# A hybrid diffusion-transformer layer: wide and narrow matmuls issued in two streams, and one PSUM pool of bank pairs for the whole program

## The chip, the cores and the metric

The kernel runs on 1 core of one Trainium2 chip, in one launch. Its time is device microseconds; the time before is the median of 3 runs, 1769.75 us (1761.52 to 1772.15). TensorE is PE in all rows (PEld is its weight load), VectorE is DVE, ScalarE is ACT, GpSimd is POOL, and SyncE, which only issues DMAs here, is SP.

## The reference, cut to what matters

One layer over 256 latent tokens of width 2048, with 256 context tokens as a prefix, all in float32:

```python
mod = silu(c) @ w_mod + b_mod                    # 6 vectors: shift, scale, gate, twice
h   = modulate(rms_norm(x), sh1, sc1)            # and hc for the context
q, zf, zb, v = split(h @ w_in[:, :4096], 4)      # HGRN2, both directions, 8 heads
o   = scan_f(q, zf, v) + scan_b(q, zb, v)        # chunkwise gated recurrence
g, sb, sc, sh, ga, gb = split(h @ w_in[:, 4096:])
y_a = rms(o) * a_norm_g * silu(g);  y_b = sb * short_conv(sc * sh)
x   = x + g1 * ((sigmoid(ga) * (y_a @ w_pa) + sigmoid(gb) * (y_b @ w_pb)) @ w_o)
a, b = split(modulate(rms_norm(x), sh2, sc2) @ w_up, 2)       # 5632 columns each
x   = x + g2 * ((silu(dwconv3x3(a) + db) * b) @ w_down)
return rms_norm(x) * final_g
```

## The kernel before

**Products in split form.** Each float32 weight block is loaded by SP into a tile `raw` (1 MB, 4 buffers, L66), and `wsplit` (L83) makes two tiles of 1024 columns of it twice: `w_hi` on ACT (L95), the weight rounded to the matmul's format, and `w_lo` on DVE (L96), what is left over. 5 buffers of each stand ahead of PE. The activations are kept split in the same way: `hx[:, k, 0]` is the high part of row tile k of h, `hx[:, k, 1]` the low part, 256 tokens each, next to each other. A product is w_hi times high, w_hi times low, and w_lo times high.

**The projections** (`proj`, L364; `proj_q`, L381, the same for q): the weights are the stationary operand, 128 x 128, and tokens move. For a row tile k and a half n of 256 columns, `mm2` (L123) issues a wide matmul, `w_hi` over high and low together (512 columns, one PSUM bank), and right behind it a narrow one, `w_lo` over the high part (256 columns), which adds to the second half of that bank. The order is thus wide, narrow, wide, narrow, in 64 matmuls for 16 row tiles and two halves. `joined` (L129) then adds the two halves of a bank: an ACT copy and a DVE addition. There are 4 projections for q, 16 for the rest of the token mixer, 16 for the gates and 44 in the FFN, and 16 of half the length on `w_pa` and `w_pb`.

**Other products.** `proj_xc` (L395) makes forget gates from narrow matmuls alone, `values` (L442) and `token_product` (L755) have the activations stationary and the weights moving. `token_product` gives the two products at the end, w_o and w_down, in 4 column quarters `cq` of 512; t is one of two tiles of 128 tokens. In the last quarter t = 0 is finished first, then the two 256-column pieces of t = 1, and `residual` (L797) adds each to x (L804, L805), squares it (L807) and takes the root for the norm (L811, L812). After w_o the norm's factor goes through a matmul into `rb` and multiplies the transposed rows (L838 to L865), after w_down it scales the output (L943 to L947), which leaves in 8 DMAs (L948).

**PSUM.** 8 banks: `psH` has 2 for small things; the other 6 change hands between pools, 6 single banks (`psA` to L629, `psB` L739 to L875, `psD` from L918) or 3 pairs (`psW` L630 to L738, `psF` L876 to L917). A pool's tile waits until what stood in its banks in the pool before has been read.

**The order of the work.** A scheduler of the framework lays out each engine's queue from the order of the code and its own timing model; each engine then runs its queue in order and waits at semaphores. SP's queue of loads is fixed by it too. The stages, by the trace: norm, modulation and first gates to about 155 us, HGRN2 with its projections to about 432 (its last group's vector work runs on beyond), the mixer's and the gates' projections to about 940, w_o to 1010, the FFN's two projections to 1517, w_down to the end. `mod_steps` (L646) runs the remaining modulation on DVE beside the mixer and the FFN, with 16 one-column products (twice, L115 `pc`).

Of the kernel before, what the change touches and what calls it, by code (L numbers as in the profile page):

```python
# [36 lines left out]
def hybrid_layer_kernel(ctx: ExitStack, tc: tile.TileContext, I, out, dbg=None):  # L37
# [17 lines left out]
    def banks(name, n):  # L55
        cm = tc.tile_pool(name=name, bufs=n, space=PSUM, reuse_waits="tile")
        return cm, cm.__enter__()

    psA_cm, psA = banks("psA", 6)

# [56 lines left out]
    def mm3(o, wl, wh, sl, sh, start, stop):  # L117
# [3 lines left out]
        mm(o, wh, sl, False, stop)  # L121

    def mm2(o, wl, wh, s, start, stop):  # L123


        mm(o, wh, s, start, False)
        mm(o[:, T:2 * T], wl, s[:, 0, :], False, stop)

# [97 lines left out]
    for i in range(2):  # L226
        for t in range(2):
            for j, part in enumerate(xts[2 * i + t]):
                nc.scalar.activation(junk, part, AF.Square, accum_out=ssq[:, j, 2 * i + t:2 * i + t + 1])
        r = rstd[:, 2 * i:2 * i + 2]  # L230
        nc.vector.tensor_tensor(out=r, in0=ssq[:, 0, 2 * i:2 * i + 2], in1=ssq[:, 1, 2 * i:2 * i + 2], op=ALU.add)
        nc.scalar.activation(r, r, AF.Sqrt, scale=1.0 / D, bias=eps_t[:])
        nc.vector.reciprocal(r, r)
        for t in range(2):
            for part in xts[2 * i + t]:
                nc.vector.tensor_scalar(out=part, in0=part, scalar1=rstd[:, 2 * i + t:2 * i + t + 1], scalar2=None, op0=ALU.mult)
            for k4 in range(4):
                pt = psA.tile([P, 4, P], F32, name="pt4", tag="acc")
                for k in range(4):
                    kk = 4 * (k4 % 2) + k  # L240
                    nc.tensor.transpose(pt[:, k, :], xts[2 * i + t][k4 // 2][:, kk * P:kk * P + P], ident[:])  # L241
                if k4 % 2:
                    nc.scalar.copy(xsT[:, 4 * k4:4 * k4 + 4, 2 * i + t, :], pt[:])
                else:
                    nc.vector.tensor_copy(xsT[:, 4 * k4:4 * k4 + 4, 2 * i + t, :], pt[:])

# [6 lines left out]
    zacc = {}  # L253
    for d, n in [(0, n) for n in range(4)] + [(1, n) for n in range(3)]:
        pool, tag = (psH, "psh") if (d, n) == (0, 0) else (psA, "acc")
        zt = pool.tile([P, 2, T], F32, name=f"zacc{d}{n}", tag=tag)
        zacc[d, n] = zt

# [105 lines left out]
    def proj(w, cols, src, kt):  # L364

        accs = []
        for i in range(len(cols)):
            acc = psW.tile([P, 2, 2, T], F32, name="acc", tag="acw")
            accs.append(acc)
# [9 lines left out]
        return accs  # L379

    def proj_q(c0):  # L381

        accs = []
        for n in range(2):
            acc = psA.tile([P, 2, T], F32, name="acc", tag="acc")
            accs.append(acc)
        for c in range(2):
            for k, hv, lv in wviews([wblock(w_in, c * 1024, 8, c0, 256)], 8):
                kk = 8 * c + k
                for n in range(2):  # L390
                    mm2(accs[n][:].rearrange("p a b -> p (a b)"), lv[:, n * P:n * P + P], hv[:, n * P:n * P + P],
                        hx[:, kk], kk == 0, kk == KD - 1)
        return accs

    def proj_xc(w, cols):  # L395

        accs = []
        for n in range(2):
            a = psA.tile([P, 2, T], F32, name=f"acx{n}", tag="acc")
            accs.append(a)  # L400
        for c in range(2):
# [8 lines left out]
    def proj_xc1(w, c0):  # L410

        acc = psA.tile([P, 2, T], F32, name="acx", tag="acc")
        for k, hv, lv in wviews([wblock(w, 0, KD, c0, P)], KD):
# [14 lines left out]
    def gate_evac(acc, dst):  # L428

        nc.scalar.activation(dst, acc[:], AF.Sigmoid)  # L430

    def q_evac(accs):
        q = gp.tile([P, 2, T], F32, name="q", tag="q", bufs=2)
        for n, acc in enumerate(accs):
            nc.scalar.copy(q[:, n, :], acc[:, 1, :])
            nc.vector.tensor_tensor(out=q[:, n, :], in0=acc[:, 0, :], in1=q[:, n, :], op=ALU.add)  # L436
        sg = g2.tile([P, 2, T], F32, name="sq", tag="qq")
# [4 lines left out]
    def values(cb):  # L442
        accs = []
        for t in range(4):
            a = psA.tile([P, 512], F32, name=f"vacc{t}", tag="acc")
            accs.append(a)
        for c4 in range(4):
            for k, hv, lv in wviews([wblock(w_in, c4 * 512, 4, 3 * AW + cb * 512, 512)], 4):
                kk = 4 * c4 + k
                for t in range(4):  # L450
                    h = hx if t < 2 else hc
                    ts = slice((t % 2) * P, (t % 2) * P + P)
                    mm(accs[t][:], h[:, kk, 0, ts], hv, kk == 0, False)
                    mm(accs[t][:], h[:, kk, 0, ts], lv, False, False)
                    mm(accs[t][:], h[:, kk, 1, ts], hv, False, kk == KD - 1)
        for t in range(4):
            nc.scalar.copy(v[:, t, cb * 512:cb * 512 + 512], accs[t][:])

# [142 lines left out]
    for g in range(4):  # L601
# [135 lines left out]
    tp_cm.__exit__(None, None, None)  # L737
    psW_cm.__exit__(None, None, None)  # L738
    psA_cm, psA = banks("psB", 6)  # L739


# [89 lines left out]
    for cq in range(4):  # L831
        accs = token_product(w_o, KD, cq, mg_part)
        norm2 = residual(accs, cq, bcast[2], tw)
        if cq == 3:
            rb = psA.tile([P, T], F32, name="rb", tag="acc")
            for t in range(2):
# [15 lines left out]
    dump("x1", x1[:])  # L852
    rbv = strided(rb[:], 0, [[0, 2], [1, T]])
    h2_hi = {}
# [19 lines left out]

    psA_cm.__exit__(None, None, None)  # L875
    psW_cm, psW = banks("psF", 3)  # L876
    yfp = ctx.enter_context(tc.tile_pool(name="yfp", bufs=1, reuse_waits="tile"))
# [38 lines left out]
    pump(1)  # L916
    psW_cm.__exit__(None, None, None)  # L917
    psA_cm, psA = banks("psD", 6)  # L918

# [18 lines left out]
    for t in range(2):  # L938
        for cq in (0, 1, 3, 2):
# [8 lines left out]
            nc.sync.dma_start(out[0, t * P:t * P + P, cs], v1)  # L948
    psA_cm.__exit__(None, None, None)

# [35 lines left out]
```

## Time and profile before

| what | us |
|---|---|
| median of 3 runs | 1769.75 |
| the profiled execution, its own time | 1774.06 |
| span of its instructions | 1772.3 |
| PE busy in it | 1731.1 |
| DVE busy | 1317.2 |
| ACT busy | 895.5 |

The profiled execution is 4.3 us above the median; its time is 1.8 us more than its span. A matmul's duration in a row is its whole way through the array, and matmuls overlap; what one costs in a stream is the distance from its start to the start of the next.

### The profile page before, as it was taken

Reading aid. Unit: us, or ns where it says so; the run is one execution under the profiler, and the core shown is the slowest. Engines: PE = TensorE matmul, PEld = TensorE weight load, DVE = VectorE, ACT = ScalarE, POOL = GpSimd, SP = SyncE. Lnnn points to the kernel's source line nnn. Section 1 sums busy time; section 2 is a strip of 40 time slices with the busy share of each in tenths; the row PEclk is TensorE's granted clock in tenths of the full one; section 3 lists DMA queues with packets and bytes.
Section 4 is the critical chain, followed back from the end, with each engine's and each line's share of the span. In section 5 each row is a group of like instructions: output and inputs, shape, how many; then the busy total and the mean of one; then the engine's idle time right before and its main releaser. Section 6 shows DMA issues by size and latency. Waiting matters only on the chain.

```text
span 1772.3 us, 25752 instructions
## 1 busy us (share of the span) xinstructions
PE 1731.1 (98%) x10391; PEld 1493.0 (84%) x10391; DVE 1317.2 (74%) x1693; ACT 895.5 (51%) x1142; POOL 21.4 (1%) x26
## 2 busy tenths in 40 slices
PE   5999999998999999999999999999999999999998
PEld 3778888997888888888888888888888888788887
DVE  4337377687988778878875588888888887877774
ACT  4227356466555444444455454444444454665653
POOL 0000000000000000000000000000000000000000
PEclk9999999999999999999999999999999999999999
DMA  9996224223677879979886367777777755566662
GB/s 334 352 329 208 95 72 119 72 96 120 223 252 253 275 245 312 323 258 327 295 292 223 119 214 238 237 231 228 233 235 237 237 193 188 166 191 192 197 191 85
DMA packets 288989, 384.96 MB, mean 217 GB/s; under 512 B 7812, under 2 KB 241581, under 8 KB 280038
## 3 DMA queue, kind: packets, MB, share of 16 engines
q1 hardware_dynamic: 287872, 379.82, 65.1%
q10 hardware_dynamic: 694, 3.24, 0.5%
q8 instruction: 81, 1.33, 0.3%
q0 software_dynamic: 304, 0.26, 0.1%
q14 instruction: 38, 0.31, 0.0%
HBM read 381.20 MB, written 2.10 MB: 216 GB/s over the span
## 4 chain that ended last, share of the span: by engine, by line
PE 97%; DVE 1%; ACT 0%; DMA 0%; issue 0%; SPq 0%; ACTq 0%
PE acc L115 56%; PE to L115 19%; PE acx L115 6%; PE vacc L115 5%; PE zacc L115 5%; PE pm L115 2%; PE ps L115 2%; PE po L115 1%; PE pt L241 1%; DMA xt<-in_x_dram 0%; DVE w_lo L96 0%; PE pc L115 0%; PE kdt L497 0%; DVE hx L112 0%; DVE cvf L902 0%
## 5 line engine op out<-in xcount | busy, mean ns | idle before, releaser
L115 PE MATMUL acc<-hx,w_hi 128*128 128x512 f32 x2560 | 911.9, 400 | 8.9 <-DVE q L436 7.0
L95 ACT ACTIVATE w_hi<-raw 128x1024 fp32r<-128x1024 f32 (+1 forms) x522 | 549.7, 1054 | 562.8 <-PE acc L115 403.7
L96 DVE TENSOR_TENSOR w_lo<-raw,w_hi 128x1024 fp32r<-128x1024 f32 (+1 forms) x521 | 633.4, 1218 | 257.6 <-ACT w_hi L95 254.9
L115 PE MATMUL acc<-hx,w_lo 128*128 128x256 f32 x2560 | 722.7, 282 | 0.0
L115 PEld LDWEIGHTS acc<-hx,w_hi 128*128 128x128 f32 x2560 | 484.5, 189 | 128.0 <-DVE q L436 7.4
L115 PEld LDWEIGHTS acc<-hx,w_lo 128*128 128x128 f32 x2560 | 487.3, 190 | 0.7
L115 PE MATMUL to<-w_hi,hx 128*128 128x512 f32 (+1 forms) x792 | 222.8, 367 | 3.7 <-DVE bv L132 3.7
L115 PEld LDWEIGHTS to<-w_hi,hx 128*128 128x128 f32 x792 | 143.6, 189 | 29.0 <-DVE bv L132 4.1
L653 DVE SCALAR_TENSOR_TENSOR macc<-raw,cst,macc 128x2048 f32<-128x2048 f32 x64 | 150.1, 2345 | 19.4 <-DMA raw<-in_w_mod_dram 14.2
L115 PE MATMUL to<-w_lo,hx 128*128 128x512 f32 (+1 forms) x396 | 145.6, 368 | 0.0
L902 DVE SCALAR_TENSOR_TENSOR cvf<-av,pf,cvf 128x189 f32<-128x189 f32 (+2 forms) x352 | 131.5, 426 | 0.0
L111 ACT ACTIVATE hx<-y 128x512 fp32r<-128x512 f32 x88 | 55.3, 630 | 86.5 <-PE to L115 86.5
L112 DVE TENSOR_TENSOR hx<-y,hx 128x512 fp32r<-128x512 f32 x88 | 60.9, 692 | 36.5 <-ACT hx L111 36.5
L115 PEld LDWEIGHTS to<-w_lo,hx 128*128 128x128 f32 x396 | 74.9, 189 | 12.1
L115 PE MATMUL to<-w_hi,mg 128*128 128x512 f32 (+1 forms) x288 | 82.0, 368 | 0.0
L115 PE MATMUL acx<-hx,w_hi 128*128 128x256 f32 x288 | 59.5, 285 | 0.0
L115 PEld LDWEIGHTS to<-w_hi,mg 128*128 128x128 f32 x288 | 51.8, 188 | 8.8
L115 PE MATMUL acx<-hc,w_hi 128*128 128x256 f32 x288 | 59.1, 286 | 0.0
L115 PE MATMUL to<-w_lo,mg 128*128 128x512 f32 (+1 forms) x144 | 52.7, 366 | 0.0
L115 PE MATMUL zacc<-hx,w_hi 128*128 128x256 f32 x224 | 51.4, 285 | 0.0
L115 PE MATMUL acc<-y_b,w_hi 128*128 128x512 f32 x128 | 47.8, 412 | 0.0
L115 PE MATMUL zacc<-hc,w_hi 128*128 128x256 f32 x224 | 47.0, 286 | 0.0
(238 smaller groups left out, 1843.8 us busy)
## 6 DMA issues: line engine op xcount, KB each, us to landing
raw<-in_w_up_dram SPq DMA_DIRECT2D x88, 1024.0 KB, 5.1
raw<-in_w_in_dram SPq DMA_DIRECT2D x81, 1024.0 KB, 5.8
raw<-in_w_mod_dram SPq DMA_DIRECT2D x64, 1024.0 KB, 6.4
raw<-in_w_down_dram SPq DMA_DIRECT2D x44, 1024.0 KB, 5.1
raw<-in_w_mod_dram SPq DMA_DIRECT2D x64, 512.0 KB, 7.3
raw<-in_w_o_dram SPq DMA_DIRECT2D x16, 1024.0 KB, 5.7
raw<-in_w_in_dram SPq DMA_DIRECT2D x24, 512.0 KB, 4.3
raw<-in_w_pa_dram SPq DMA_DIRECT2D x8, 1024.0 KB, 5.7
```

The lines of the kernel that those rows point to most:

```text
L95: nc.scalar.activation(hi[:, :n], half, AF.Copy)
L96: sub.tensor_tensor(out=lo[:, :n], in0=half, in1=hi[:, :n].bitcast(F32), op=ALU.subtract)
L111: nc.scalar.activation(dst[0], src, AF.Copy)
L112: nc.vector.tensor_tensor(out=dst[1], in0=src, in1=dst[0].bitcast(F32), op=ALU.subtract)
L115: return nc.tensor.matmul(o, lhsT, rhs, start=start, stop=stop, skip_group_check=True)
L241: nc.tensor.transpose(pt[:, k, :], xts[2 * i + t][k4 // 2][:, kk * P:kk * P + P], ident[:])
L653: nc.vector.scalar_tensor_tensor(out=acc[:], in0=raw[:], scalar=cst[:, k, 0:1], in1=acc[:], op0=ALU.mult, op1=ALU.add)
L902: nc.vector.scalar_tensor_tensor(out=c4[:, ro, co], in0=a4[:, ri, ci], scalar=pf[:, tap * NF + f:tap * NF + f + 1], in1=c4[:, ro, co], op0 ...
```

## The change

`proj` takes the row tiles four at a time (one `w_hi` and one `w_lo` tile): first the 8 wide matmuls of the four, then the 8 narrow ones. `proj_q` goes, q comes from `proj` and is joined by one ACT copy and one DVE addition in place of two each. The five pools of 6 banks become one pool of three pairs for the whole program; every tile that had a bank of its own is now one half of a pair (or a pair with one half unused).

```diff
-    psA_cm, psA = banks("psA", 6)
+    psW = ctx.enter_context(tc.tile_pool(name="psW", bufs=3, space=PSUM))
+    def bank_pair(name):
+        return psW.tile([P, 2, 512], F32, name=name, tag="acw")
...
-                    for k, hv, lv in islice(view, 4):
-                        kk = 8 * c + k
-                        for n in range(2):
-                            mm2(acc[:, n].rearrange("p a b -> p (a b)"), lv[:, n * P:n * P + P], hv[:, n * P:n * P + P],
-                                src[:, kk], kk == 0, kk == kt - 1)
+                    part = list(islice(view, 4))
+                    for k, hv, lv in part:
+                        for n in range(2):
+                            mm(acc[:, n], hv[:, n * P:n * P + P], src[:, 8 * c + k], c == 0 and k == 0, False)
+                    for k, hv, lv in part:
+                        for n in range(2):
+                            mm(acc[:, n, T:2 * T], lv[:, n * P:n * P + P], src[:, 8 * c + k, 0, :], False, 8 * c + k == kt - 1)
...
+        slots = [bank_pair("to")] + ([bank_pair("to")] if cq == 3 else [])
+        slots = [pair[:, i] for pair in slots for i in range(2)]
         for t in range(2):
             for i, cs in enumerate(pieces(cq, t)):
-                a = psA.tile([P, 512], F32, name=f"to{t}{i}", tag="acc")
-                accs[t, i] = a[:, :cs.stop - cs.start]
+                accs[t, i] = slots[t + i][:, :cs.stop - cs.start]
...
-        q = q_evac(proj_q(256 * g))
+        q = q_evac(proj(w_in, [256 * g], hx, KD)[0])
...
-    psA_cm.__exit__(None, None, None)
-    psW_cm, psW = banks("psW", 3)
```

The other lines of the diff give the start's transposes (`pt4`), the first gates (`zacc`), `proj_xc`, `values` and `rb` their halves of pairs in the same way, and take out the other changes of pools. The queues of SP and POOL hold the same work in the same order before and after.

Three places of the queues follow; a number behind a name tells buffers apart, `[waits ...]` names the engines whose semaphores a row waits for.

PE before, from the last projection of q (`acc_3897`, `acc_3898`, one bank each) to the first of the mixer (`acc_4242`):

```order
L115 MATMUL acc_3897<-hx_97,w_hi_3963 128x512
L115 MATMUL acc_3897<-hx_97,w_lo_3964 128x256
L115 MATMUL acc_3898<-hx_97,w_hi_3963 128x512
L115 MATMUL acc_3898<-hx_97,w_lo_3964 128x256
L115 MATMUL acc_4242<-hx_97,w_hi_4245 128x512 [waits DVE_49]
L115 MATMUL acc_4242<-hx_97,w_lo_4246 128x256
```

PE after, the same place (`acc_3869` is q, `acc_4207` the mixer's first):

```order
L114 MATMUL acc_3869<-hx_97,w_hi_3934 128x512 x8
L114 MATMUL acc_3869<-hx_97,w_lo_3935 128x256 x8
L114 MATMUL acc_4207<-hx_97,w_hi_4210 128x512 [waits Activation_49]
L114 MATMUL acc_4207<-hx_97,w_hi_4210 128x512 x7
L114 MATMUL acc_4207<-hx_97,w_lo_4211 128x256 [waits DVE_49]
L114 MATMUL acc_4207<-hx_97,w_lo_4211 128x256 x7
```

Wide and narrow stand in eights. The first matmul of the mixer waited before for DVE's addition of q, which frees the bank; now it waits for its `w_hi`, and the wait for DVE at its narrow ones is for `w_lo`.

PE before, from the last FFN projection (`acc_13271`) to w_down (`to00` is t = 0, `to10` is t = 1 of the first quarter):

```order
L115 MATMUL acc_13271<-hx_97,w_lo_13337 128x256
L115 MATMUL to00_13373<-w_hi_13377,hx_97 128x512 [waits DVE_49,Activation_49]
L115 MATMUL to00_13373<-w_lo_13378,hx_97 128x512
L115 MATMUL to00_13373<-w_hi_13377,hx_97 128x512 [waits DVE_49]
L115 MATMUL to10_13374<-w_hi_13377,hx_97 128x512 [waits DVE_49]
```

PE after, the same place (`to_13322` is the pair of both):

```order
L114 MATMUL acc_13224<-hx_97,w_lo_13290 128x256 x7
L114 MATMUL to_13322<-w_hi_13325,hx_97 128x512 [waits Activation_49]
L114 MATMUL to_13322<-w_lo_13326,hx_97 128x512 [waits DVE_49]
L114 MATMUL to_13322<-w_hi_13325,hx_97 128x512 [waits DVE_49]
L114 MATMUL to_13322<-w_hi_13325,hx_97 128x512
```

The wait at the first matmul of t = 1, for DVE's addition of the last FFN projection (`bv`), is gone; the three that are left are for operands (the split y, and `w_lo`).

DVE before, at the end of the program (`to_14672` is t = 0, `to_14673` and `to_14674` the two pieces of t = 1):

```order
L804 TENSOR_TENSOR res<-to_14672,bc 128x512 [waits PE_49]
L805 TENSOR_TENSOR x_8116<-x_8116,res 128x512 [waits DVE_49]
L812 RECIPROCAL r_8118<-r_8118 128x1 [waits Activation_49]
L945 TENSOR_SCALAR x_8116<-x_8116,r_8118 128x512 [waits DVE_49]
L943 SCALAR_TENSOR_TENSOR x_8116<-x_8116,r_8118,fg 128x512
L804 TENSOR_TENSOR res<-to_14673,bc 128x256 [waits PE_49]
L805 TENSOR_TENSOR x_8116<-x_8116,res 128x256 [waits DVE_49]
```

DVE after, the same place (t = 0 and the first piece of t = 1 are the halves of one pair):

```order
L780 TENSOR_TENSOR res<-to,bc 128x512 [waits PE_49]
L780 TENSOR_TENSOR res<-to,bc 128x256
L781 TENSOR_TENSOR x_8077<-x_8077,res 128x512 [waits DVE_49]
L781 TENSOR_TENSOR x_8077<-x_8077,res 128x256 [waits DVE_49]
L780 TENSOR_TENSOR res<-to,bc 128x256 [waits DVE_49,PE_49]
L781 TENSOR_TENSOR x_8077<-x_8077,res 128x256 [waits DVE_49]
L788 RECIPROCAL r_8079<-r_8079 128x1 [waits Activation_49]
```

Before, the row of t = 0 waits for t = 0's last matmul and runs its whole course to the scaled output ahead of t = 1. After, its one wait stands for both halves of the pair, so that it comes when the first piece of t = 1 is done too. The end of w_o has the same two orders.

## Rows read from the trace of the kernel before

**Rows 1.** The page, part 1: PE's busy time, share of the span, instructions.

```profile
PE   1731.1 (98%) x10391; PEld 1493.0 (84%) x10391; DVE 1317.2 (74%) x1693; ACT 895.5 (51%) x1142; POOL 21.4 (1%) x26
```

**Rows 2.** The page, part 4: the chain that ended last, by line.

```profile
PE acc L115 56%; PE to L115 19%; PE acx L115 6%; PE vacc L115 5%; PE zacc L115 5%; PE pm L115 2%; PE ps L115 2%; PE po L115 1%; PE pt L241 1%; DMA xt<-in_x_dram 0%; DVE w_lo L96 0%; PE pc L115 0%; PE kdt L497 0%; DVE hx L112 0%; DVE cvf L902 0%
```

**Rows 3.** The page, part 5: count, busy us, mean ns, idle before and releaser.

```profile
L115 PE MATMUL acc<-hx,w_hi 128*128 128x512 f32 x2560 | 911.9, 400 | 8.9 <-DVE q L436 7.0
L115 PE MATMUL acc<-hx,w_lo 128*128 128x256 f32 x2560 | 722.7, 282 | 0.0
```

**Rows 4.** Windows, tile acc alone, in the FFN: PE busy and its instructions.

```profile
1100.00:1200.00 100.00, 100.00 (x568) 86.71 (x567) 5.74 (x9) 4.55 (x8) 1.00 0.69 226
```

**Rows 5.** Timeline of PE in the FFN: start us, us, instruction.

```profile
1199.68 0.40 PE L115 MATMUL acc<-hx,w_hi 128*128 128x512 f32 x1
1199.92 0.28 PE L115 MATMUL acc<-hx,w_lo 128*128 128x256 f32 x1
1200.03 0.40 PE L115 MATMUL acc<-hx,w_hi 128*128 128x512 f32 x1
```

**Rows 6.** Timeline of PE in w_down, wide matmuls alone.

```profile
1754.26 0.61 PE L115 MATMUL to<-w_hi,hx 128*128 128x512 f32 x2
...
1758.34 0.50 PE L115 MATMUL to<-w_hi,hx 128*128 128x512 f32 x2
```

**Rows 7.** Timeline of PE in a forget gate's projection, narrow matmuls alone.

```profile
339.76 0.28 PE L115 MATMUL acx<-hc,w_lo 128*128 128x256 f32 x1
...
342.28 0.28 PE L115 MATMUL acx<-hx,w_lo 128*128 128x256 f32 x1
```

**Rows 8.** Waits of PE: us in total, times, longest us.

```profile
PE acc L115 <- DVE q L436: 7.0, 1, 7.0
...
PE to L115 <- DVE bv L132: 3.7, 1, 3.7
```

**Rows 9.** Timeline of PE at the mixer's first projection.

```profile
439.57 0.80 PE L115 MATMUL acc<-hx,w_hi 128*128 128x512 f32 x1 [7.03 <-DVE q L436]
...
440.38 0.63 PE L115 MATMUL acc<-hx,w_hi 128*128 128x512 f32 x1
...
441.02 0.63 PE L115 MATMUL acc<-hx,w_hi 128*128 128x512 f32 x1
```

**Rows 10.** Timeline of DVE, same place.

```profile
439.10 0.41 DVE L436 TENSOR_TENSOR q<-acc,q 128x256 f32<-128x256 f32 x1
```

**Rows 11.** Windows: PE, PEld, DVE, ACT, POOL busy, granted clock, DMA share, GB/s.

```profile
437.50:444.40 6.90, 4.83 (x15) 4.16 (x16) 6.90 (x8) 2.79 (x3) 0.00 (x0) 0.51 0.74 265
...
1523.00:1526.40 3.40, 3.40 (x10) 2.62 (x9) 2.64 (x8) 1.26 (x2) 0.00 (x0) 0.50 0.00 1
...
638.90:645.70 6.80, 6.80 (x24) 5.93 (x24) 4.12 (x5) 2.00 (x3) 2.32 (x2) 0.50 0.12 40
```

**Rows 12.** Windows: the same columns, from q's end through the last HGRN2 group.

```profile
432.00:540.00 108.00, 100.97 (x665) 87.10 (x664) 99.07 (x117) 61.71 (x79) 0.00 (x0) 0.97 0.72 242
```

**Rows 13.** Timeline of DVE at the end of the program.

```profile
1758.77 0.69 DVE L804 TENSOR_TENSOR res<-to,bc 128x512 f32<-128x512 f32 x1 [5.96 <-PE to L115]
...
1763.08 0.42 DVE L804 TENSOR_TENSOR res<-to,bc 128x256 f32<-128x256 f32 x1 [0.43 <-PE to L115]
```

**Rows 14.** Timeline of ACT at the end of the program.

```profile
1760.22 0.63 ACT L807 ACTIVATE sq<-x 128x512 f32<-128x512 f32 x1 [8.67 <-DVE x L805]
...
1760.98 0.30 ACT L811 ACTIVATE r<-ssq 128x1 f32<-128x1 f32 x1
...
1766.56 1.33 ACT L947 ACTIVATE x<-x,r 128x512 f32<-128x512 f32 x2 [0.23 <-DVE r L812]
```

**Rows 15.** Timeline of ACT, then of PE, behind w_o.

```profile
1012.16 0.29 ACT L811 ACTIVATE r<-ssq 128x1 f32<-128x1 f32 x1
...
1015.35 0.80 PE L115 MATMUL acc<-hx,w_hi 128*128 128x512 f32 x1 [1.84 <-DVE hx L865]
```

**Rows 16.** Timeline of PE, the one-column products of the modulation.

```profile
635.74 3.93 PE L115 MATMUL pc<-ones_r,macc 128*128 128x1 f32 x32
```

More of the change, by code (lines that the diff above doesn't have):

```diff
@@ L237, in hybrid_layer_kernel @@
             for k4 in range(4):
-                pt = psA.tile([P, 4, P], F32, name="pt4", tag="acc")
+                if k4 % 2 == 0:
+                    pt4 = bank_pair("pt4")
+                pt = pt4[:, k4 % 2].rearrange("p (k e) -> p k e", k=4)
                 for k in range(4):
@@ L242, in hybrid_layer_kernel @@
                 if k4 % 2:
-                    nc.scalar.copy(xsT[:, 4 * k4:4 * k4 + 4, 2 * i + t, :], pt[:])
+                    nc.scalar.copy(xsT[:, 4 * k4:4 * k4 + 4, 2 * i + t, :], pt)
                 else:
-                    nc.vector.tensor_copy(xsT[:, 4 * k4:4 * k4 + 4, 2 * i + t, :], pt[:])
+                    nc.vector.tensor_copy(xsT[:, 4 * k4:4 * k4 + 4, 2 * i + t, :], pt)
     to_cols(pa[:, 32:121], rows_a[:89, :], 89)
@@ L253, in hybrid_layer_kernel @@
     zacc = {}
[L254 to L257, printed above, removed]
+    for i, (d, n) in enumerate([(0, 0), (0, 1), (0, 2), (0, 3), (1, 0), (1, 1), (1, 2)]):
+        if i == 0:
+            zt = psH.tile([P, 512], F32, name="zacc00", tag="psh")[:]
+        else:
+            if i % 2:
+                pair = bank_pair("zacc")
+            zt = pair[:, 1 - i % 2]
+        zacc[d, n] = zt.rearrange("p (a b) -> p a b", a=2)
     NB = KD // 2
@@ L364, in proj @@
     def proj(w, cols, src, kt):
[L366 to L369, printed above, removed]
+        accs = [bank_pair("acc") for _ in cols]
         for c in range(kt // 8):
@@ L373, in proj @@
                 for acc, view in zip(accs, views):
-                    for k, hv, lv in islice(view, 4):
-                        kk = 8 * c + k
+                    part = list(islice(view, 4))
+                    for k, hv, lv in part:
                         for n in range(2):
-                            mm2(acc[:, n].rearrange("p a b -> p (a b)"), lv[:, n * P:n * P + P], hv[:, n * P:n * P + P],
-                                src[:, kk], kk == 0, kk == kt - 1)
-        return accs
-    def proj_q(c0):
-        accs = []
-        for n in range(2):
[L385 to L393, printed above, removed]
+                            mm(acc[:, n], hv[:, n * P:n * P + P], src[:, 8 * c + k], c == 0 and k == 0, False)
+                    for k, hv, lv in part:
+                        for n in range(2):
+                            mm(acc[:, n, T:2 * T], lv[:, n * P:n * P + P], src[:, 8 * c + k, 0, :], False, 8 * c + k == kt - 1)
+        return [acc[:].rearrange("p n (s t) -> p n s t", s=2) for acc in accs]
     def proj_xc(w, cols):
[L397 to L400, printed above, removed]
+        pair = bank_pair("acx")
+        accs = [pair[:, n].rearrange("p (a b) -> p a b", a=2) for n in range(2)]
         for c in range(2):
@@ L410, in proj_xc1 @@
     def proj_xc1(w, c0):
-        acc = psA.tile([P, 2, T], F32, name="acx", tag="acc")
+        acc = bank_pair("acx")[:, 0].rearrange("p (a b) -> p a b", a=2)
         for k, hv, lv in wviews([wblock(w, 0, KD, c0, P)], KD):
@@ L428, in gate_evac, with q_evac @@
     def gate_evac(acc, dst):
-        nc.scalar.activation(dst, acc[:], AF.Sigmoid)
-    def q_evac(accs):
+        nc.scalar.activation(dst, acc, AF.Sigmoid)
+    def q_evac(acc):
         q = gp.tile([P, 2, T], F32, name="q", tag="q", bufs=2)
-        for n, acc in enumerate(accs):
-            nc.scalar.copy(q[:, n, :], acc[:, 1, :])
-            nc.vector.tensor_tensor(out=q[:, n, :], in0=acc[:, 0, :], in1=q[:, n, :], op=ALU.add)
+        joined(q[:], acc)
         sg = g2.tile([P, 2, T], F32, name="sq", tag="qq")
@@ L442, in values @@
     def values(cb):
[L443 to L446, printed above, removed]
+        pairs = [bank_pair("vacc") for _ in range(2)]
+        accs = [pairs[t // 2][:, t % 2] for t in range(4)]
         for c4 in range(4):
@@ L452, in values @@
                     ts = slice((t % 2) * P, (t % 2) * P + P)
-                    mm(accs[t][:], h[:, kk, 0, ts], hv, kk == 0, False)
-                    mm(accs[t][:], h[:, kk, 0, ts], lv, False, False)
-                    mm(accs[t][:], h[:, kk, 1, ts], hv, False, kk == KD - 1)
+                    mm(accs[t], h[:, kk, 0, ts], hv, kk == 0, False)
+                    mm(accs[t], h[:, kk, 0, ts], lv, False, False)
+                    mm(accs[t], h[:, kk, 1, ts], hv, False, kk == KD - 1)
         for t in range(4):
-            nc.scalar.copy(v[:, t, cb * 512:cb * 512 + 512], accs[t][:])
+            nc.scalar.copy(v[:, t, cb * 512:cb * 512 + 512], accs[t])
     def hgrn(g, ft, q):
@@ L834, in hybrid_layer_kernel @@
         if cq == 3:
-            rb = psA.tile([P, T], F32, name="rb", tag="acc")
+            rb = bank_pair("rb")[:, 0, 0:T]
             for t in range(2):
@@ L852, in hybrid_layer_kernel @@
     dump("x1", x1[:])
[L853 removed]
+    rbv = strided(rb, 0, [[0, 2], [1, T]])
     h2_hi = {}
```

13 lines of the change are left out of this document (removed).

## The prediction

> **What bounds the kernel now.** I read the page from the top, then the chain, then the groups, and only then single stretches. PE is busy for 1731.1 us, 98% of the span [rows 1], so what counts is how closely its matmuls follow each other, and the few places where it stands still. The chain of work that ended last says the same: 56% of the span is PE on the tile acc, the projections; the next is `to`, w_o and w_down, with 19% [rows 2]. The groups show what acc is made of: as many wide matmuls (512 columns) as narrow ones (256), 2560 of each on hx, to which come 256 of each on y_a and y_b: 2816 pairs [rows 3]. The mean durations there, 400 and 282 ns, are no prices, since matmuls overlap. The price is the distance of starts. In the timeline a wide one starts at 1199.68, its narrow one at 1199.92, the next wide one at 1200.03: 240 and 110 ns here, 350 together [rows 5]. Over 100 us of the FFN, 568 acc matmuls, that is 284 pairs, fill PE without a gap: 352 ns a pair [rows 4].
>
> Two streams of one width stand in the same trace. In w_down 18 wide matmuls lie between 1754.26 and 1758.34 (six turns of w_hi twice and w_lo once): 4.08 us, 227 ns each [rows 6]. In a forget gate's projection, where the weights stand in the array as in `proj`, 21 narrow ones lie between 339.76 and 342.28 (seven turns of three): 120 ns each [rows 7]. Sum: 347 ns, five less than a pair costs in the alternating order.
>
> The waits of PE come last. Of those that the change touches, the mixer's first projection waits 7.0 us for DVE's addition of q, and w_down 3.7 us for DVE's addition of bv, once each [rows 8].
>
> **The streams.** A half of a block, 4 row tiles by 2 halves, is 8 pairs. Before: 8 x 352 = 2817 ns. After: 8 x 227 + 8 x 120 = 2774 ns, and one change of width in each direction, for which I keep the 5 ns of one alternating pair: 2779 ns. 38 ns a half block, and 2816 / 8 = 352 of them: **13.4 us**. Bounds: above, without the cost of the changes, 43 ns or 15.2 us. Below, a wide matmul with weights standing and hx moving is shown in no stream; in rows 5 it took 240 ns. Should it keep the 233 that is left of a pair of 352 beside a narrow one of 119, the 8 + 8 cost 8 x 353 and nothing is gained: 0. I take 13.4, as wide and narrow matmuls of the other stages keep their price whatever stands in the array. Of the joins, q's two copies and two additions become one each, on engines that are ahead of PE: nothing on the path.
>
> The Trainium skill has a rule against this term. "TensorE: Matmul & The Clock Gate", section "Back-to-back issue gap", gives a matmul at the upper clock its columns over 2.4 GHz plus about 2.5 ns, whatever its neighbour is. By it a pair costs 325 ns as an estimate from that page, in either order, and this term is 0. The trace differs in size (352 and 347 [rows 4, 6, 7]), and in that a wide matmul costs 227 behind a wide one and 240 behind a narrow one [rows 5, 6].
>
> **The wait for q.** Before, the mixer's first projection takes banks in which q has just been summed. PE stands for 7.03 us until 439.57, when DVE's second addition, which started at 439.10 behind other work in its queue, is over [rows 9, 10]. Then the clock is low: 0.51 of full speed, the 1.2 GHz level, from 437.50 to 444.40, in which PE worked 4.83 us [rows 11]; a pair takes from 440.38 to 441.02, 0.64 us, where 0.35 is usual [rows 9]. Half of 4.83 is 2.4 us. After the change the three pairs turn in one order: the mixer's first projection gets the pair of a forget gate, which was read long before, and the order shows only waits for its own w_hi and w_lo. Gain 7.0 + 2.4 = **9.4 us**. What is late next is DVE: from 432 to 540 it is busy for 99.07 of 108 us [rows 12]. Take 9.4 out, and some 1 us for the streams (1.4% of the projections in it), and some 98 us are left for 99 of DVE's work. Five buffers of w_lo, worth 8 x 347 ns each, stand between, 14 us; and the narrow eight, which alone need w_lo, now come 8 x 227 = 1.8 us behind the wide. So I let nothing be given back; the lower bound is half, 4.7.
>
> **The wait for bv.** The same at w_down: the second accumulator takes a bank of the last FFN projection, which DVE frees 3.7 us late [rows 8]; then the clock is at 0.50 from 1523.00 to 1526.40 with PE busy throughout [rows 11], 1.7 us lost. After, the pair of the FFN's projection before it is taken, and the waits that are left are for split parts of y that are made in order, ahead of PE. Gain **5.4 us**, at least 2.7.
>
> **What the pairs cost.** The residual of t = 0 in a last quarter waits for both halves of its pair. At the end of the program it started at 1758.77; now it starts with the first piece of t = 1, at 1763.08 in the old time [rows 13]. Then ACT has to do, between there and the end, what it did under PE's last matmuls: DVE's two products and the first addition take some 1.7 us to 1764.8, then ACT squares t = 0 (0.63 and about 0.2 to read its sum), takes the root (0.30), squares the first piece (0.6), scales a quarter of t = 0 (half of 1.33, 0.67), squares the second piece (0.6), scales (0.67), takes the root (0.30), waits 0.2 for the reciprocal, and scales twice (1.33): the sum is 1764.8 + 5.5 = 1770.3, where it was 1766.56 + 1.33 = 1767.9 [rows 14]. With some overlap I take **+2.2 us**, between 1 and 3; the stores behind it are as before. Behind w_o the same chain has no scaling in it. The last root ended there at 1012.16 + 0.29 = 1012.45 and PE went on at 1015.35 [rows 15]; what comes ahead of it now is the square and the root of t = 0, 0.63 + 0.2 + 0.30 = 1.1 us, of which a little lies beside DVE's work: **+0.9 us**, between 0 and 2.5 if the low clock behind it lasts longer. At the start the second half of a pair of transposes waits until the first is copied: 8 copies of about 0.69 us, the size of a 512-column read of PSUM on DVE [rows 13], are 5.5 at most and 0 at least; three pairs turn, so that one's copy lies under the others' transposes: **+0.5**.
>
> **The sum.** -13.4 - 9.4 - 5.4 + 2.2 + 0.9 + 0.5 = -24.6 us. Against the profiled execution, 1774.06, that is 1749.5; this one was 4.3 us over the median of the runs, so against that 1769.75 - 24.6 = 1745. Range of this case: 1737 (15.2, 9.4, 5.4, with +1) to 1753.
>
> **Rivals.**
> (1) Width doesn't matter to the pace, as by the page's rule, or a wide stream with weights standing is no faster. Against it: rows 6 and 7; for it: no such stream in the trace. Then -14.8 + 3.6 = -11.2: 1758.5. Chance 0.16.
> (2) The two waits go and others take their places: DVE, nearly full in that stretch [rows 12], is late with w_lo, and the splits of y with w_down. For it: PE's standing still was what let DVE catch up. Against: five buffers. Then -13.4 + 3.6 = -9.8: 1760. Chance 0.10.
> (3) Slower: the clock. From 635.74 PE ran 3.93 us of one-column products without a gap [rows 16], and at 638.90 the clock fell to 0.50 for 6.8 us though PE never stood idle [rows 11]: thin work can lower it. Should streams of narrow matmuls do the same, each such stretch costs half of 6.8, 3.4 us; the streams' and waits' 24.6 are gone with the eighth, and a dozen make 1745 + 41 = 1786. Against it: the gates' narrow streams run at full pace, 120 ns, for much longer than eight matmuls [rows 7]. Chance 0.03.
> That the change does not do what it says is ruled out by the order, where eights of each width stand.
>
> **How the numbers follow.** The forecast has 0.71, the rivals 0.16, 0.10 and 0.03. 1% of the time, 17.7 us, is about what a measurement here can tell from no change. Faster by more than that means below 1752: nearly all of the forecast (0.68), and that part of rivals 1 and 2 in which only some of the gain is lost (0.07), 0.75. Within 1%: the rest of these, 0.21. Slower: 0.04. The range runs from 1736, the forecast's lower end with a little for the scatter of medians, to 1761, just beyond rivals 1 and 2.
>
> **What would show it.** Streams: the windows of acc in the FFN hold about 576 matmuls in 100 us in place of 568; wide ones 227 and narrow ones 120 ns apart. A wide one at 235 or more decides for rival 1. Waits: no row of PE for q or bv, no half clock at 437 and 1523; new rows that name w_lo or hx there are rival 2. Pairs: the last scaling on ACT ends about 2 us later behind PE's last matmul. Half-clock stretches inside projections, beyond the ones behind one-column products and behind w_o, would be rival 3. If PE's gaps are gone and the time is still above 1760, the price per matmul is wrong.

## The result and the profile after

In the same session the changed kernel took 1752.9 us (median of 7 runs, 1751.69 to 1753.69), the kernel before 1769.75 (7 runs, 1761.52 to 1772.33): a ratio of 0.9916, with a 95% interval of 0.9893 to 0.9939. It is faster by 16.9 us, where 24.6 were forecast. Each kernel's own scatter turned out to be the clue: the new one's runs lie within 2 us, the old one's within 11.

The page, part 1 (PE) and part 5, of the changed kernel; the columns are those of [rows 1] and [rows 3]:

```profile
PE   1717.2 (98%) x10391; PEld 1490.5 (85%) x10391; DVE 1310.5 (75%) x1689; ACT 896.2 (51%) x1140; POOL 20.5 (1%) x26
...
L114 PE MATMUL acc<-hx,w_hi 128*128 128x512 f32 x2560 | 646.3, 394 | 1.8 <-DVE hx L841 1.8
...
L114 PE MATMUL acc<-hx,w_lo 128*128 128x256 f32 x2560 | 358.9, 283 | 0.0
```

PE does the same 10391 instructions and is still the bound. The mean durations are as before (394 and 283 for 400 and 282), and the busy times of the two groups fell by some 630 us together only because a group's busy time counts matmuls that overlap once, and in a stream matmuls of one group overlap each other. They say nothing on the gain. The pace does: the window of [rows 4], and a wider one, in the changed kernel, tile acc alone:

```profile
1100.00:1200.00 100.00, 100.00 (x573) 87.97 (x573) 6.16 (x9) 5.12 (x9) 1.00 0.72 236
1030.00:1430.00 400.00, 400.00 (x2295) 352.05 (x2293) 25.22 (x37) 20.47 (x36) 1.00 0.71 232
```

In the kernel before the wide window reads as follows:

```profile
1030.00:1430.00 400.00, 400.00 (x2266) 346.94 (x2265) 24.61 (x36) 20.44 (x36) 1.00 0.71 232
```

A window counts the matmuls that its borders cut, too, so the distance of starts is the better measure. The timeline of PE in the changed kernel, merged by form:

```profile
1100.42 2.00 PE L114 MATMUL acc<-hx,w_hi 128*128 128x512 f32 x8
1102.26 1.12 PE L114 MATMUL acc<-hx,w_lo 128*128 128x256 f32 x8
1103.22 0.63 PE L114 MATMUL acc<-hx,w_hi 128*128 128x512 f32 x2
```

Eight wide ones take 1.84 us (230 each), eight narrow ones 0.96 (120 each), and the eight pairs 2.80: each whole half block in that wide window has 2793 or 2794 ns from its first start to the next one's, 349.2 a pair. In the kernel before, a pair takes 353.3 ns on the mean, in a cycle of three pairs (349, 350 and 361). In single matmuls the eight wide ones read 233, 236, 228, 232, 231, 227, 227, 227: only behind the fifth do they settle at the price that I read in w_down.

The waits of PE in the changed kernel, the longest first (us in total, times, longest); all but the last are those of the start:

```profile
PE pt L206 <- DMA rows_c<-in_c_ctx_dram: 6.9, 1, 6.9
PE pt L206 <- DMA ct<-in_ctx_dram: 4.6, 1, 4.6
PE pt L236 <- DVE xt L229: 3.2, 1, 3.2
PE zacc L114 <- ACT hx L110: 3.0, 1, 3.0
PE acc L114 <- DVE hx L841: 1.8, 1, 1.8
```

The rows for q and bv [rows 8] are gone, and nothing stands in their place. Windows of the changed kernel around the two old waits and over the stretch of [rows 12] (columns as in [rows 11]):

```profile
427.00:441.00 14.00, 14.00 (x82) 12.32 (x81) 14.00 (x13) 11.91 (x12) 0.00 (x0) 1.00 0.45 149
1495.00:1502.50 7.50, 7.50 (x42) 6.51 (x41) 7.50 (x12) 5.49 (x9) 0.00 (x0) 1.00 0.53 173
432.00:540.00 108.00, 108.00 (x718) 93.70 (x717) 106.22 (x118) 65.80 (x80) 0.00 (x0) 1.00 0.80 268
```

PE is busy throughout at the full clock. DVE is busy for 106.22 of 108 us, more than before, and still in time. The tail of the changed kernel, on PE, DVE and ACT:

```profile
1740.25 0.28 PE L114 MATMUL to<-w_hi,hx 128*128 128x256 f32 x1
...
1739.13 1.02 DVE L780 TENSOR_TENSOR res<-to,bc 128x512 f32<-128x512 f32 x2 [10.28 <-PE to L114]
...
1744.27 1.34 ACT L919 ACTIVATE x<-x,r 128x512 f32<-128x512 f32 x2 [0.23 <-DVE r L788]
```

The residual of t = 0 now starts 1.12 us ahead of PE's last matmul; before, it was 5.43 (1758.77 [rows 13] against the last start on PE, 1764.20). From that last start to the end of the span there are 10.3 us, before 8.1.

### The profile page after: what moved, and what is told of

Read it like the earlier page. It is cut to its first block, busy times and chain, and to the rows that moved or that the text cites. A ratio compares the mean times of both kernels' runs of the same rounds, so it can differ in the third digit from the quotient of the medians.

```text
span 1750.6 us, 25743 instructions
## 1 busy us (share of the span) xinstructions
PE 1717.2 (98%) x10391; PEld 1490.5 (85%) x10391; DVE 1310.5 (75%) x1689; ACT 896.2 (51%) x1140; POOL 20.5 (1%) x26
## 4 chain that ended last, share of the span: by engine, by line
PE 98%; ACT 1%; DVE 1%; DMA 0%; issue 0%; ACTq 0%
PE acc L114 57%; PE to L114 19%; PE acx L114 6%; PE vacc L114 5%; PE zacc L114 5%; PE pm L114 2%; PE ps L114 2%; PE po L114 1%; PE pt L236 1%; PE pc L114 0%; DMA rows_a<-in_norm_g_dram 0%; ACT hx L222 0%; PE kdt L476 0%; ACT sq L783 0%; PE ptx L821 0%
## 5 line engine op out<-in xcount | busy, mean ns | idle before, releaser
L114 PE MATMUL acc<-hx,w_hi 128*128 128x512 f32 x2560 | 646.3, 394 | 1.8 <-DVE hx L841 1.8
L114 PEld LDWEIGHTS acc<-hx,w_hi 128*128 128x128 f32 x2560 | 461.9, 189 | 85.0 <-DVE hx L841 2.0
L114 PEld LDWEIGHTS acc<-hx,w_lo 128*128 128x128 f32 x2560 | 350.5, 191 | 25.4
L114 PE MATMUL acc<-hx,w_lo 128*128 128x256 f32 x2560 | 358.9, 283 | 0.0
L114 PEld LDWEIGHTS acx<-hc,w_hi 128*128 128x128 f32 x288 | 45.3, 191 | 0.8
```

The source lines that it names most:

```text
L114: return nc.tensor.matmul(o, lhsT, rhs, start=start, stop=stop, skip_group_check=True)
```

## The experiments

**Each half of the change alone, and the old kernel again.** The first question was why one kernel scatters and the other doesn't. The first four kernels ran on one chip, beside 19 runs of the kernel before (1761.74 to 1773.28, median 1764.79).

Streams alone, in the old pools:

```
 before.py, proj (proj_q in the same way)
-for k, hv, lv in islice(view, 4):
-    for n in range(2):
-        mm2(acc[:, n] ..., lv[...], hv[...], src[:, kk], kk == 0, kk == kt - 1)
+part = list(islice(view, 4))
+for k, hv, lv in part:
+    for n in range(2):
+        mm(acc[:, n] ..., hv[...], src[:, 8 * c + k], c == 0 and k == 0, False)
+for k, hv, lv in part:
+    for n in range(2):
+        mm(acc[:, n, 1, :], lv[...], src[:, 8 * c + k, 0, :], False, 8 * c + k == kt - 1)
```

> The kernel before with the two streams alone (eight wide, then eight narrow matmuls in every half block, for q too), in its old pools. Theory 1 (rhythm): the alternating order has no fixed price; a pair costs 347 or 353 ns by the rhythm that PE falls into behind a wait or a change of clock, and that is why the kernel before scatters over 10 us; streams cost 349 a pair each time. Then: every half block 2793 ns, fast runs within 3 us of each other, PE's waits for q (7.0) and bv (3.7) still there, about 1752.9 + 9.4 + 5.4 - 2.2 (the tail is as before) = 1765.5. Theory 2 (width): each alternating pair costs 353 because its width changes; the same 1765.5, but a scatter as large as before, since that comes from the waits. Rival on the waits: if the streams and not the pool took them away, 1751.

Measured: 1765.46 (10 runs, 1764.29 to 1766.55), ratio 0.9993 (0.9975 to 1.001). The streams alone gain nothing against the median of before; what they do is hold the time within 2.3 us. Both waits stay, in the waits of PE of this kernel:

```profile
PE acc L115 <- DVE q L442: 7.4, 1, 7.4
...
PE to L115 <- DVE bv L132: 3.9, 1, 3.9
```

The pool alone:

```
 after.py, proj
-part = list(islice(view, 4))
-for k, hv, lv in part:
+for k, hv, lv in islice(view, 4):
     for n in range(2):
         mm(acc[:, n], hv[...], src[:, 8 * c + k], c == 0 and k == 0, False)
-for k, hv, lv in part:
-    for n in range(2):
         mm(acc[:, n, T:2 * T], lv[...], src[:, 8 * c + k, 0, :], False, 8 * c + k == kt - 1)
```

> The changed kernel with its matmuls in the old alternating order: the pool alone. Both theories: no wait of PE for q or bv, the tail as in the changed kernel. Theory 1 (rhythm): stretches at 347 and stretches at 353 ns a pair, whichever they fall into: a scatter of up to 10 us between 1748 and 1765. Theory 2 (width): 353 everywhere, 4.3 x 2816 = 12 us over the changed kernel, 1765, with little scatter.

Measured: 1757.04 (10 runs, 1748.4 to 1763.53), ratio 0.9947 (0.9924 to 0.997). The scatter stays, as theory 1 had it, and its lower end lies below every run of the changed kernel. Neither q nor bv is among its waits.

The kernel before once more, without an edit:

> The kernel before once more, for a second profiled execution of the same instructions. Theory 1 (rhythm): other stretches at 347 and 353 ns than in the first profile; if this execution is near 1762, most of the FFN runs at 347, if it is near 1772, at 353. Theory 2 (width): the same pace at the same places in both profiles, and what differs in time is the wait for q, 7.0 in the first.

Measured: 1763.34 (one run). The waits for q and bv are again 7.0 and 3.7 us, so the 10.7 us between this execution and the first profile are not theirs. Most of them are in the pace: the FFN alone, from its first to its last matmul on acc, takes 501.9 us in the first profile and 493.8 in the second, with 6.8 us of low clock at its start in both. Of the rest a part is the clock: behind the one-column products near 640 the first profile has 6.8 us of low clock [rows 11], and the second has none:

```profile
638.90:645.70 6.80, 6.80 (x45) 6.10 (x45) 4.36 (x7) 2.33 (x3) 2.33 (x2) 1.00 0.24 83
```

Windows on tile acc: first the old kernel's first profile, then its second, then the pool alone:

```profile
650.00:750.00 100.00, 100.00 (x567) 86.69 (x567) 8.20 (x12) 6.86 (x12) 1.00 0.93 317
785.00:885.00 100.00, 100.00 (x579) 88.19 (x578) 7.51 (x11) 6.83 (x12) 1.00 0.91 313
```

```profile
650.00:750.00 100.00, 100.00 (x578) 87.41 (x578) 8.21 (x12) 6.81 (x12) 1.00 0.94 329
785.00:885.00 100.00, 100.00 (x567) 86.72 (x566) 8.20 (x12) 6.83 (x12) 1.00 0.90 312
1030.00:1430.00 400.00, 400.00 (x2310) 352.69 (x2309) 25.31 (x37) 20.99 (x37) 1.00 0.72 237
```

```profile
650.00:750.00 100.00, 100.00 (x568) 86.76 (x567) 7.51 (x11) 6.59 (x12) 1.00 0.91 316
785.00:885.00 100.00, 100.00 (x579) 87.43 (x578) 8.20 (x12) 6.81 (x12) 1.00 0.90 308
1030.00:1430.00 400.00, 399.40 (x2305) 351.95 (x2304) 25.29 (x37) 20.97 (x37) 1.00 0.70 232
```

The same instructions run at two paces: 567 or 578 matmuls in 100 us, a pair at 353.3 or at 346.7 ns, all at a granted clock of 1.00. Between two breaks in these long stretches the pace holds; behind three of the breaks (the one-column products near 640 and 775, the waits behind w_o near 1010) it came out differently in these three profiles. Not every break is open in this way: from 565 to 627, and in the last 170 pairs of the FFN, all three profiles run at 353.3. At the better pace the timeline of the second profile shows each pair of the FFN alike, 0.23 and 0.11 to 0.12 us, where [rows 5] has 0.24 and 0.11:

```profile
1199.53 0.39 PE L115 MATMUL acc<-hx,w_hi 128*128 128x512 f32 x1
1199.76 0.28 PE L115 MATMUL acc<-hx,w_lo 128*128 128x256 f32 x1
1199.87 0.39 PE L115 MATMUL acc<-hx,w_hi 128*128 128x512 f32 x1
```

That is theory 1. From 1021 to 1449 the FFN runs 1206 pairs without a break; 1206 x 6.7 ns = 8.1 us, the FFN's 8.0 above. It fits what the runs of the kernel before show in all sessions: of 55, 34 lie between 1760.9 and 1766.3 (median 1764.2) and 21 between 1769.5 and 1776.3 (median 1772.2), 8 us apart and none between. The two profiled executions, 1774.06 and 1763.34, are one of each group. What makes a break end in the one pace or the other was not found. The length of the low clock does not: behind 6.8 us of it the first profile runs at 353.3 from 646 and from 1021, and at 346.7 from 783.

**What a change of width costs.** Streams of a whole block: the loop over halves goes, and all eight row tiles are issued wide, then narrow.

> The changed kernel with streams of a whole block: sixteen wide, then sixteen narrow matmuls. If what a stream costs over 347 ns a pair is paid in the first matmuls behind a change of width (2793 - 8 x 347 = 17 ns for each eight pairs), half of it goes: 8.5 x 352 = 3.0 us, 1750, and 348 ns a pair in the FFN. If it is paid on every wide matmul (230 in place of 227), the time stays at 1752.9 and the pace at 349.

Measured: 1752.06 (4 runs, 1750.75 to 1753.03). Its blocks have 5567 ns between their starts, 347.9 a pair: what is paid for is the change, not each wide matmul. It is the change of width and not that of the tile: in [rows 6] and [rows 7] w_hi and w_lo take turns at one width, and cost 227 and 120 ns throughout. In time the 3 us don't show: against the changed kernel's profile 1.7 are gained from the first projection on acc to w_o, and 2.2 are lost from there to the 256th matmul of the FFN; the sixteens with banks apart, below, show where. Then sixteens of which every second block begins with the width that the last one ended with:

```
 after.py, proj, instead of the two halves
+part = list(view)
+for wide in ((True, False), (False, True))[c % 2 if kt == KD else 0]:
+    for k, hv, lv in part:
...
```

> The changed kernel with streams of a whole block, 16 matmuls, in which every second block begins with the width that the block before ended with (wide, narrow, narrow, wide). Theory (a stream costs 346.7 ns a pair, and each change of width there and back 20 ns more): one change there and back in 32 pairs in place of one in 8, 347.3 ns a pair; of the 352 x 20 ns = 7.0 us that the eights pay 1.8 are left: 5.2 us less than the changed kernel, 1747.7. Rival (the price hangs on the first matmuls of a block of weights, whatever stands before them): 348 a pair as with plain sixteens, 1752.

Measured: 1750.18 (4 runs, 1748.28 to 1750.48). The pace is the theory's to the nanosecond; timeline of PE in the FFN:

```profile
1200.28 7.44 PE L114 MATMUL acc<-hx,w_hi 128*128 128x512 f32 x32
1207.56 4.00 PE L114 MATMUL acc<-hx,w_lo 128*128 128x256 f32 x32
1211.40 7.44 PE L114 MATMUL acc<-hx,w_hi 128*128 128x512 f32 x32
```

32 pairs take 11.12 us from start to start (11113 ns in most). With 2793 for eight and 5567 for sixteen, all three are 346.7 ns a pair and 20 ns for a change there and back. In time some 2.5 of the 5.2 us expected are missing again.

> The changed kernel with streams of two: both wide matmuls of a row tile, then both narrow ones. If each change there and back costs its 20 ns in full, 346.7 + 10 = 357 ns a pair, 1752.9 + 2816 x 7.6 ns = 1774. If the cost builds up over the five wide matmuls behind a change, less: between 347 and 353. If the rhythm decides, stretches at two paces.

Here the two loops over n stand inside the loop over k. Measured: 1749.12 (one run), 348.3 ns a pair in every stretch looked at. Neither the full price nor two paces: more changes of width than with eights, and yet no dearer.

> The changed kernel in alternating order, but every second half block begins with the narrow one, so that two of one width meet at each border. Theory (the rhythm stays what a break made it, and a border is such a break): the borders are the same sequence of instructions each time, so one pace holds throughout, either 347 or 353 (1747 or 1765). Rival (a rhythm changes only with a wait or the clock): stretches at both paces, as in the pool alone, changing at the one-column products and behind w_o.

The edit: the pair's two matmuls change places in every second half block. Measured: 1754.9 (one run), 349.8 ns a pair. Neither theory as I put it: half blocks take 2781, 2779, 2813 and 2821 ns in turn, two at the one pace and two at the other, in all stretches. The borders stand in this timeline of PE (x2 is a border, from 1101.84 on wide, narrow, wide, narrow, wide):

```profile
1101.84 0.62 PE L114 MATMUL acc<-hx,w_hi 128*128 128x512 f32 x2
...
1104.77 0.40 PE L114 MATMUL acc<-hx,w_lo 128*128 128x256 f32 x2
...
1107.46 0.64 PE L114 MATMUL acc<-hx,w_hi 128*128 128x512 f32 x2
...
1110.37 0.40 PE L114 MATMUL acc<-hx,w_lo 128*128 128x256 f32 x2
...
1113.03 0.62 PE L114 MATMUL acc<-hx,w_hi 128*128 128x512 f32 x2
```

From wide to narrow 2.93 us and then 2.91, from narrow to wide 2.69 and then 2.66: the slower two halves stand on both sides of the narrow border at 1104.77, the faster two on both sides of the one at 1110.37. So a border of two wide matmuls turns the pace into the other one (at 144 of the 145 such borders whose two sides can be told), and a border of two narrow ones leaves it (at all 139). Why two wide ones turn it was not found.

**The tail, and a better kernel.** The changed kernel with banks apart in the last quarters:

```
 after.py, token_product
-slots = [bank_pair("to")] + ([bank_pair("to")] if cq == 3 else [])
-slots = [pair[:, i] for pair in slots for i in range(2)]
+if cq < 3:
+    pair = bank_pair("to")
+    slots = [pair[:, 0], pair[:, 1]]
+else:
+    alone = psH.tile([P, 512], F32, name="to", tag="psh")
+    slots = [alone[:], bank_pair("to")[:, 0], bank_pair("to")[:, 0]]
```

> The changed kernel, but in the last quarter of w_o and of w_down t = 0 sums in a bank of its own (of psH), and the two pieces of t = 1 in a pair each. Theory (the pair delays t = 0's residual): the last matmul of PE is followed by 8.1 us in place of 10.3, and rb comes 1.2 us sooner behind w_o: 2.2 + 1.2 = 3.4 us less, 1749.5. Rival (the tail is longer for the order on ACT, not for the pair): 10.3 us stay, 1752.9.

Measured: 1749.8 (4 runs, 1749.76 to 1751.7). In its timeline the residual starts ahead of PE's last matmul again, and the span ends 8.1 us behind that, at 1748.0:

```profile
1734.50 0.69 DVE L784 TENSOR_TENSOR res<-to,bc 128x512 f32<-128x512 f32 x1 [5.96 <-PE to L114]
...
1739.93 0.28 PE L114 MATMUL to<-w_hi,hx 128*128 128x256 f32 x1
```

The 2.2 us are the pair's. The other half of the theory failed: behind w_o the first part of rb comes 0.45 us sooner, but the FFN waits for the second, and from the first matmul of w_o to the FFN's first there are 97.3 us, in the changed kernel 97.2. That the time came out near the 1749.5 of the theory is in part luck.

> The changed kernel with the turned streams of sixteen and with the last quarters' banks apart, the two edits that each gained alone. If they add up: 3.1 us (banks apart) and 5.2 us (1.84 ns on 2816 pairs) under the changed kernel, 1744.6; with the low clock behind w_o in its longer form, 1746. Rival (what the streams gain is given back at the waits and the clock behind w_o): 1748, as each edit alone.

Measured: 1748.98 (6 runs, 1747.06 to 1749.99). The rival. A row of PE's waits shows where: two waits for hx behind w_o, 3.2 us, where the changed kernel has one of 1.8:

```profile
PE acc L114 <- DVE hx L847: 3.2, 2, 1.8
```

and in the timeline of that stretch PE takes four wide matmuls and stands again:

```profile
1001.08 1.20 PE L114 MATMUL acc<-hx,w_hi 128*128 128x512 f32 x4 [1.84 <-DVE hx L847]
1003.60 1.22 PE L114 MATMUL acc<-hx,w_hi 128*128 128x512 f32 x2 [1.33 <-DVE hx L847]
```

The first four use up the two row tiles of the FFN's input that DVE has split by then, and PE stands for 1.3 us until it has split the third; the low clock lasts 6.8 us there in place of 3.4. This is not a matter of sixteens alone: the streams alone, with eights, have the second wait too.

```profile
PE acc L115 <- DVE hx L871: 3.1, 2, 1.8
```

The changed kernel has another order there. The FFN's first two projections run side by side, and the scheduler laid 14 wide matmuls of both ahead of the first narrow one, so that the first two row tiles serve eight: the fifth wide matmul starts at 1005.30, and the third row tile is split at 1006.32.

```profile
1003.85 5.07 PE L114 MATMUL acc<-hx,w_hi 128*128 128x512 f32 x14 [1.84 <-DVE hx L841]
1008.76 1.11 PE L114 MATMUL acc<-hx,w_lo 128*128 128x256 f32 x8
1009.71 0.63 PE L114 MATMUL acc<-hx,w_hi 128*128 128x512 f32 x2
1010.18 1.10 PE L114 MATMUL acc<-hx,w_lo 128*128 128x256 f32 x8
```

> The changed kernel with streams of two and with the last quarters' banks apart. Theory (streams of two keep 348.3 ns a pair in every execution, without a rhythm of their own): 0.8 ns x 2816 = 2.3 us and 3.1 us less than the changed kernel, 1747.5, fast runs within 3 us. Rival (they fall into two rhythms like the alternating order): a scatter of 5 us or more.

Measured: 1747.79 (6 runs, 1747.08 to 1747.94), as the theory had it; these streams go on by row tile and don't wait there.

> The changed kernel once more, on the chip of the two others. Theory (streams of eight have one rhythm): 1752 to 1754, every half block 2793 ns, where the kernel before again lies at 1762 to 1766 or at 1770 to 1773, by the rhythm of its FFN. Rival (the changed kernel has two rhythms as well, and has only shown one): a scatter of 5 us or more.

Measured: 1753.05 (6 runs, 1751.68 to 1753.51), ratio 0.9919 (0.9891 to 0.9946): one pace.

> The kernel with turned streams of sixteen and the banks apart, but with the first two projections of the FFN, which run while h2 is still being split, in streams of two. Theory (sixteen wide matmuls in a row use up h2's row tiles faster than DVE makes them: a second wait of 1.3 us and 3.4 us more of the low clock, 3.0 us in all): the second wait for hx is gone, the time 3 us under that of sixteens with banks apart, 1746. Rival (the low clock behind w_o is as long as it is by chance, and the wait is hidden anyway): 1749 again.

`if len(cols) == 2:` takes the loops of two, all other projections the turned sixteens. Measured: 1746.12 (6 runs, 1744.58 to 1747.74), ratio 0.9882 (0.9855 to 0.991). The second wait is gone:

```profile
PE acc L114 <- DVE hx L856: 1.8, 1, 1.8
```

This is the fastest kernel of the study: 6.9 us under the changed one (measured on another chip), 18.4 under the median of before in its session (1764.56).

## Why the prediction was right, and what in it was wrong

The direction was right, and the time lies in the range. The sum was 7.7 us off (16.9 for 24.6), and the fault is in one term: the pool's terms came out at 12.4 us for 11.2, as worked out below, which leaves 4.5 for the streams, where 13.4 were forecast. The size of the gain is partly luck. Four of the seven runs of the kernel before fell into its upper group, and the median with them; against the lower group's 1764.2 the gain is 11.3 us, and in the session in which the changed kernel was measured again it was 12.4 (1765.48 less 1753.05). The lower end of "this case", 1737, was added up wrongly, too: its terms give 29.0 us, 1740.8; nothing hangs on it.

**The streams: the step that failed is "Before: 8 x 352".** I took the distance of starts in one stretch of one execution for the price of the alternating order. It is one of two. Against 353.3 the streams gain 4.2 ns a pair, 12 us on 2816 pairs, close to the 13.4; against 346.7 they lose 2.5 ns, 7 us. On the first profile, where some 470 pairs ran at the better pace, that makes -8.6 us (2342 x 4.2 less 474 x 2.5); on the median of before in the second session it is 0 (streams alone, 0.9993). Against the better pace my lower bound of 0 was too high. The proof lay in the trace that I had: from 785 to 885 the old kernel does 579 matmuls on acc in 100 us, in alternating order and with one width beside the other. I had opened only the FFN's windows. The change of width, for which I kept 5 ns, costs 20; that alone is 352 x 15 ns = 5.3 us of the term. (The second wide matmul of an eight reads 236 ns, over the 235 that I had set as a sign for rival 1; the mean of the eight is 230.)

Rival 1 (width doesn't matter to the pace) is therefore nearer in its number than the forecast: its 11.2 us from the lower group's 1764.2 give 1753.0. Its reason is not what the runs show: the order of widths does matter to the pace, only not in one direction. The rule of the Trainium skill that I weighed ("TensorE: Matmul & The Clock Gate", section "Back-to-back issue gap") came near in the same way, in that a price without regard to the neighbour makes the term 0. But that section gives the formula as the gap of an isolated matmul, and I read it as a price in a stream; its 325 ns a pair appear in no run here, where the least is 346.7.

**The two waits: right.** Both are gone, with the half clock behind them, and DVE, of which I said that little was left, gave nothing back. Against the streams alone, at one pace of the projections, the changed kernel gains 9.4 us from the first projection on acc to the 512th pair, and 5.8 us from the end of the FFN into w_down: 9.4 and 5.4 were forecast. The pool's whole effect can be read in the same way, though on two chips: streams in the old pools 1765.46, streams in the new 1753.05, 12.4 us; my terms for it were -9.4 - 5.4 + 2.2 + 0.9 + 0.5 = -11.2.

**The pairs: right in size.** The tail's +2.2 is 10.3 less 8.1, and it goes when the banks are apart. From the first matmul of w_o to the FFN's first there are 97.2 us, before 96.6: 0.6 for my 0.9, and this part stays when the banks are apart (97.3), so it is not shown to be the pair's. At the program's start the first projection on acc begins 2.5 us later, for which I had 0.5; 1.7 of it is a low clock near 35 us that lasted 6.8 us in this execution and 3.4 in the other, which the kernel before shows at both lengths too.

**The rest between the two profiled executions.** Spans 1772.3 and 1750.6: -21.7. The terms as measured are -9.4 and -5.8 (waits), -8.6 (streams), +2.2, +0.6 and +2.5 (pairs and start). Three low stretches became shorter, 6.8 to 3.4 us. The first of them in the kernel before stands in [rows 11]; here are the other two, and then the three in the changed kernel, the clock third from the end:

```profile
775.40:782.20 6.80, 6.80 (x24) 5.93 (x25) 1.82 (x3) 1.12 (x2) 2.29 (x2) 0.50 0.21 72
1014.40:1021.20 6.80, 5.85 (x18) 4.96 (x19) 6.80 (x12) 6.80 (x12) 0.00 (x0) 0.50 0.01 2
```

```profile
632.30:635.70 3.40, 3.40 (x14) 3.02 (x13) 1.26 (x2) 1.26 (x2) 1.05 (x2) 0.50 0.01 2
765.40:768.80 3.40, 3.40 (x13) 2.95 (x13) 0.00 (x0) 1.06 (x1) 1.54 (x2) 0.50 0.01 4
1004.40:1007.80 3.40, 3.40 (x9) 2.69 (x9) 3.40 (x6) 3.40 (x7) 0.00 (x0) 0.50 0.00 0
```

They are those behind the one-column products and behind w_o, and give -5.1. In the two behind the one-column products the change is not shown to have a part: the first is missing in the old kernel's second profile, and the second lasts 3.4 us there and 6.8 in the changed kernel's own repeat. Behind w_o it may have one: the low stretch there lasted 6.8 us in both profiles of the kernel before and in the streams alone, and 3.4 in the changed kernel, its repeat and the pool alone; but it lasted 6.8 in the run of the borders as well, in the new pool, so no run settles it. Together -23.6; 1.9 us of loss stay unplaced.

**Rival 2** fell for this kernel in the two places that it named, and came true elsewhere in another: in the kernel with sixteens, and with eights in the old pools, the FFN's input was late behind w_o. **Rival 3** fell: no half clock in any stretch of projections beyond those behind one-column products and w_o.

## What to carry to other kernels

Before you price an order of instructions from one stretch, look up the same loop in every stage of the trace and, if you can, in a second execution: a kernel whose runs fall into two groups may be running the same code at two paces, and a median of seven runs then says how many fell on each side. Order matmuls so that their pace doesn't hang on what went before; here twos by row tile and long streams both did that, and the gain over the better half of the old runs came from freed waits, not from the pace. Where one pool replaces several, look for the tile whose reader now waits for its neighbour: 2.2 us at the end of the program hung on one bank.

## What the runs showed of the hardware that was not expected

- The same alternating matmuls (512 and 256 columns) run at 346.7 or 353.3 ns a pair at a granted clock of 1.00, for up to 1206 pairs without a change, in different executions of one program. The pace changed at breaks only: waits, the clock, other matmuls between, or two wide ones in a row. Two wide ones in a row turned it into the other pace at 144 of 145 borders, two narrow ones at none of 139.
- Wide matmuls behind narrow ones settle at 227 ns from the sixth on (233, 236, 228, 232, 231 before); 8, 16 and 32 pairs in streams take 2793, 5567 and 11113 ns, that is 346.7 each and 20 ns for the change there and back. Streams of two, with four times as many changes as eights, take 348.3 a pair, so the 20 ns don't add up when changes lie close.
- The clock's low stretch (granted 0.50, the 1.2 GHz level) behind the same one-column products lasted 6.8, 3.4 or 0 us in different executions, with PE busy each time.
